# Wide row-maximum folds, maxima scaled on ScalarE, output weights that carry the sub-norm gains, and other buffer counts in a hybrid attention block

## The chip, the core and the metric

The kernel runs on one core of a Trainium2 chip. The metric is the device time of one launch in microseconds (us). Five engines work side by side, each through its own queue in order: TensorE (PE; its weight loads are shown apart as PEld), VectorE (DVE), ScalarE (ACT), GpSimd (POOL) and SyncE (SP), whose queue issues nearly all DMAs of this kernel. An engine whose next instruction waits holds up everything behind it in its queue.

## What is computed

One decoder layer on x (2048 tokens by 1024). h = RMSNorm(x), and one input projection of h is split into three attention branches and a gate z:

```
proj = rms_norm(x, norm_g) @ w_in
cq, ckv, kr, dq, dk, dv, mq, z = split(proj)
y_mla  = latent attention, 8 heads, 64 + 32 rotary columns, causal
y_diff = differential attention, 4 heads of two causal maps each:
         o = (softmax(q1 k1) - lam * softmax(q2 k2)) v
         y_diff = rms_norm(o, diff_subln_g) * (1 - lam_init)
y_mem  = attention over 256 memory tokens, 4 heads
x + (concat(y_mla, y_diff, y_mem) * silu(z)) @ w_out
```

Everything is float32 in the reference. The kernel keeps most operands as two float16 parts (a high part and what is left), so that a product takes three matmuls.

## The kernel before

The 2048 tokens are 16 tiles of 128, in 4 blocks of 4 tiles. The work is cut into steps: "m" (memory attention, 4 blocks), "d" (differential attention, 2 groups of 2 heads by 4 blocks) and "a" (latent attention, 4 groups of 2 heads by 4 blocks). A step has a preparation (projection, norms, rotary embedding, high and low parts, transposes by DMA) and the attention maps. A map goes over key tiles j: score matmuls into the PSUM tile `st`, Exp on ScalarE into the float32 tile `p32` (L493), the low part of it on VectorE into `plo` (L494), and then probability-by-value matmuls that read the upper halves of `p32` (L503, L505) and, one key tile later, `plo` (L523). `p32` has 3 buffers and `plo` has 4.

Softmax needs a maximum per query row that is subtracted. It isn't exact here: `est_block` computes scores of the high parts alone, takes row maxima of them, and puts the maximum divided by -32 as one more column into the query tile `qs` (L408), which is transposed a second time into `qB` (L471, L886). For block 0 the maximum is reduced straight from PSUM (L389). For blocks 1 to 3 ScalarE copies each score tile to bfloat16, the first key chunk into `er` (L391), the others into `ec` (L394), VectorE takes the running maximum (L395), and after every two query tiles folds 512 columns down to 64 by three halvings (L399) and reduces these (L400). `er` is two query tiles wide, with two buffers; `ec` has three.

The sources of all DMA transposes share one tag `s2`, 6 buffers (the function `stack`): the high and low parts of x, the query and key parts `qa`, `s`, `ks`, `qs` and the latents. The transposed queries `qB` have 5 buffers. Scratch tiles of 4 KB per partition share the tag `t4` with 2 buffers (`tmp4`); they go round in the order in which the program asks for them. `rope_tables` takes two of them, after three small tiles of its own for the positions and frequencies, which its first DMA (L254) fills.

After a "d" step `post_d` normalises the 64 columns of each head: squares on ScalarE with sums (L583), (sum + eps)^-0.5 on GpSimd (L97, L101), the product with it (L588) and with the gain row `g_sub` (L589), and then the gate (L592). `load_wout` loads w_out in 8 chunks of 128 rows, scales it by 64 and splits it in high and low parts (L926, L927); chunks 4 and 5 hold the rows of the "d" branch.

What sets the order: the generators of preparations, fillers and attention units are interleaved by due times, and each instruction gets a priority from that. A scheduler then lays the instructions of each engine in the order of a simulated run, in which a tile is handed out when a buffer of its tag is free. So the order on an engine depends on the durations in that simulation, and buffer counts change the order.

Of the kernel before, what the change touches and what calls it, by code (L numbers as in the profile page):

```python
# [11 lines left out]
F32 = mybir.dt.float32  # L12
F16 = mybir.dt.float16
BF16 = mybir.dt.bfloat16
I32 = mybir.dt.int32
# [4 lines left out]
P = 128  # L20
# [7 lines left out]
WS = 64.0  # L28
# [4 lines left out]
def _bc(ap, axis, n):  # L33
    ap = ap.unsqueeze(axis)
    shape = list(ap.shape)
    shape[axis] = n
    return ap.broadcast_to(shape)
# [3 lines left out]
def hybrid_block(ctx: ExitStack, tc: tile.TileContext, x, mem, positions, norm_g, w_in, mla_q_norm_g,  # L41
# [14 lines left out]
    ps_v = ctx.enter_context(tc.tile_pool(name="ps_v", bufs=1, space=bass.MemoryType.PSUM))  # L56

    def stack(shape, name):
        return wk.tile(shape, F16, tag="s2", name=name, bufs=6)

    def bigt(shape, name):
        return big.tile(shape, F16, tag="big", name=name)
# [20 lines left out]
    def gain_row(src, n, name):  # L83
        t = cst.tile([P, n], F32, name=name)
        SP.dma_start(t, src.broadcast_to([P, n]))
        return t
# [4 lines left out]
    def rstd_of(ss, shape, name, tag="rstd"):  # L91
        r = sm.tile([P, 32 if tag == "rstd" else 8], F32, tag=tag, name=name)
        n = int(np.prod(shape))
        rv = r[:, 0:n]
        if len(shape) == 2:
            rv = rv.rearrange("p (a b) -> p a b", b=shape[1])
        G.tensor_scalar(rv, ss, EPS, None, ALU.add)  # L97
        m = mhalf
        if len(shape) == 2:
            m = m.unsqueeze(2)  # L100
        G.tensor_tensor(rv, rv, m.broadcast_to([P] + list(shape)), ALU.pow)  # L101
        return rv
# [88 lines left out]
    def tmp4(name):  # L191
        return wk.tile([P, 1024], F32, tag="t4", name=name, bufs=2)
# [57 lines left out]
    sin_t = cst.tile([P, NT, 16], F32, name="sin_t")  # L250

    def rope_tables():
        pos_i = wk.tile([P, NT], I32, tag="posi", name="pos_i")
        SP.dma_start(pos_i, positions[0].rearrange("(t p) -> p t", p=P))  # L254
        pos_f = wk.tile([P, NT], F32, tag="posf", name="pos_f")
        V.tensor_copy(pos_f, pos_i)
        inv = np.float32(10000.0) ** (-np.arange(0, 32, 2, dtype=np.float32) / np.float32(32))
        inv_t = wk.tile([P, 16], F32, tag="invt", name="inv_t")
        for i in range(16):
            G.memset(inv_t[:, i:i + 1], float(inv[i]))  # L260
        w1 = tmp4("rp1")
        w2 = tmp4("rp2")
        ang = w1[:, 0:256]
        k = w1[:, 256:512]
        h = w1[:, 512:768]
        r = w1[:, 768:1024]
        a3 = ang.rearrange("p (t f) -> p t f", f=16)
        V.tensor_tensor(a3, _bc(pos_f, 2, 16), _bc(inv_t, 1, NT), ALU.mult)
        magic = 12582912.0
        V.tensor_scalar(k, ang, 1.0 / math.pi, magic, ALU.mult, ALU.add)  # L270
        V.tensor_scalar_sub(k, k, magic)
        p1 = 201.0 / 64.0
        p2 = math.pi - p1
        e2 = 2.0 ** (math.floor(math.log2(p2)) - 10)
        p2 = math.floor(p2 / e2) * e2
        p3 = math.pi - p1 - p2
        V.scalar_tensor_tensor(r, k, -p1, ang, ALU.mult, ALU.add)
        V.scalar_tensor_tensor(r, k, -p2, r, ALU.mult, ALU.add)
        V.scalar_tensor_tensor(r, k, -p3, r, ALU.mult, ALU.add)
        V.tensor_scalar(h, k, 0.5, -0.25, ALU.mult, ALU.add)  # L280
        V.tensor_scalar_add(h, h, magic)
        V.tensor_scalar_sub(h, h, magic)
        V.scalar_tensor_tensor(h, h, -2.0, k, ALU.mult, ALU.add)
        V.tensor_scalar(h, h, -2.0, 1.0, ALU.mult, ALU.add)
        V.scalar_tensor_tensor(w2[:, 0:256], r, -1.0, r, ALU.mult, ALU.max)
        A.activation(w2[:, 256:512], r, AF.Sin)
        A.activation(w2[:, 512:768], w2[:, 0:256], AF.Sin, scale=-1.0, bias=halfpi)
        V.tensor_tensor(sin_t.rearrange("p t f -> p (t f)"), w2[:, 256:512], h, ALU.mult)
        V.tensor_tensor(cos_t.rearrange("p t f -> p (t f)"), w2[:, 512:768], h, ALU.mult)
# [4 lines left out]
    g_k = gain_row(mla_kn_g, 96, "g_k")  # L294
    g_n = cst.tile([P, 64], F32, name="g_n")
    V.tensor_tensor(g_n, g_q[:, 0:64], g_k[:, 0:64], ALU.mult)
    g_sub = gain_row(diff_subln_g, 64, "g_sub")
    V.tensor_scalar_mul(g_sub, g_sub, (1.0 - LAM_INIT) / WS)
    lamw = tmp4("lamw")
    lamt = lamw[:, 0:128].rearrange("p (a b) -> p a b", b=32)  # L300
    SP.dma_start(lamt.rearrange("p a b -> p (a b)"), diff_lambda.rearrange("o a b -> o (a b)").broadcast_to([P, 128]))
# [72 lines left out]
    def est_block(st, i, nmap, mcol, lhs, rhs):  # L374
        b = st.b
        mx = sm.tile([P, nmap, 4, 2], F32, tag="mx", name=f"mx{i}_{st.name}", bufs=2)
        fold = b >= EB
        for m in range(nmap):
            for t in range(4):
                if fold and t % 2 == 0:  # L380
                    er = wk.tile([P, 2, 512], BF16, tag="er", name="er", bufs=2)
                for c in range(b + 1):
                    ps = ps_e.tile([P, 512], F32, tag="pe", name="pe")
                    n = (4 if c < b else t + 1) * P
                    T.matmul(ps[:, 0:n], lhsT=lhs(m, t), rhs=rhs(m, c, n // P), start=True, stop=c < b)  # L385
                    if c == b:
                        T.matmul(ps[:, t * P:n], lhsT=ident, rhs=mask_e, start=False, stop=True)  # L387
                    if not fold:
                        V.reduce_max(mx[:, m, t, c:c + 1], ps[:, 0:n], axis=AX.X)  # L389
                    elif c == 0:  # L390
                        A.activation(er[:, t % 2], ps, AF.Copy)  # L391
                    else:
                        ec = wk.tile([P, 512], BF16, tag="ec", name="ec", bufs=3)
                        A.activation(ec[:, 0:n], ps[:, 0:n], AF.Copy)  # L394
                        V.tensor_tensor(er[:, t % 2, 0:n], er[:, t % 2, 0:n], ec[:, 0:n], ALU.max)  # L395
                    yield 0.5
                if fold and t % 2:
                    for n in (256, 128, 64):
                        V.tensor_tensor(er[:, :, 0:n], er[:, :, 0:n], er[:, :, n:2 * n], ALU.max)  # L399
                    V.reduce_max(mx[:, m, t - 1:t + 1, 0], er[:, :, 0:64], axis=AX.X)  # L400
        if b == 1 and not fold:
            mr = sm.tile([P, nmap * 4], F32, tag="mr", name=f"mr{i}_{st.name}", bufs=2)
            V.reduce_max(mr, mx.rearrange("p m t c -> p (m t) c"), axis=AX.X)
            mr = mr.rearrange("p (m t) -> p m t", t=4)
        else:
            mr = mx[:, :, :, 0]
        for m in range(nmap):
            V.tensor_scalar_mul(mcol(m), mr[:, m, :], -1.0 / MS)  # L408


    def prep_d(st, units):
# [63 lines left out]
    class Map:  # L475
# [9 lines left out]
        def head(self, j):  # L485
            t0 = max(0, j - self.diag0)
            n = (4 - t0) * P
            ps = ps_s.tile([P, 512], F32, tag="st", name="st")
            self.scores(ps, j, t0, n, j >= self.diag0)
            p32 = wk.tile([P, 512], F32, tag="p32", name="p32", bufs=3)  # L490
            plo = wk.tile([P, 512], F16, tag="plo", name="plo", bufs=4)
            phi = p32.bitcast(BF16).rearrange("p (n t) -> p n t", t=2)[:, :, 1]
            A.activation(p32[:, :n], ps[:, :n], AF.Exp, scale=self.scale)  # L493
            V.tensor_tensor(plo[:, :n], p32[:, :n], phi[:, :n], ALU.subtract)  # L494
            return t0, phi, plo
# [81 lines left out]
    def post_d(st, y):  # L577
        y8 = y.rearrange("p t h d -> p (t h) d")
        ss = sm.tile([P, 8], F32, tag="yss", name=f"yss_{st.name}")
        ys = new_ys(4 + st.g, st.b)  # L580
        sink = ys[:, 0].rearrange("p t k -> p (t k)")
        for i in range(8):
            A.activation(sink[:, 64 * i:64 * i + 64], y8[:, i, :], AF.Square, scale=1.0 / 8.0, accum_out=ss[:, i:i + 1])  # L583
        yield 1.0
        r = rstd_of(ss[:, 0:8], [8], f"yr_{st.name}", "rstd_y")
        yield 1.0
        yield 1.0
        V.tensor_tensor(y8, y8, _bc(r, 2, 64), ALU.mult)  # L588
        V.tensor_tensor(y8, y8, _bc(g_sub, 1, 8), ALU.mult)  # L589
        yield 1.0  # L590
        yf = y.rearrange("p t h d -> p t (h d)")
        V.tensor_tensor(yf, yf, st.z, ALU.mult)  # L592
        yield 1.0
        yield from finish(st, yf, 4 + st.g, ys)
# [325 lines left out]
    def load_wout(cs):  # L920
        for c in cs:
            f = wk.tile([P, 1024], F32, tag="f4", name=f"f_wo{c}", bufs=2)
            SP.dma_start(f, w_out[0, c * P:(c + 1) * P, :])
            yield 1.0
            wt = bigt([P, 2, 1024], f"wo{c}")
            A.activation(wt[:, 0, :], f, AF.Copy, scale=WS)  # L926
            V.scalar_tensor_tensor(wt[:, 1, :], f, WS, wt[:, 0, :], ALU.mult, ALU.subtract)  # L927
            wout[c] = wt
            yield 1.0

# [318 lines left out]
```

## Time and profile before

| what | value |
|---|---|
| time, median of 3 runs | 1398.42 us (1397.34 to 1401.3) |
| time of the profiled execution | 1403.92 us |
| its span, first to last instruction | 1402.0 us |
| instructions | 35085 |
| busy PE / DVE / ACT / POOL | 93% / 79% / 64% / 25% |
| mean granted TensorE clock | 0.978 |
| chain that ended last, by engine | PE 59%, DVE 13%, DMA 10%, POOL 6%, ACT 5% |

Busy shares are of the span. Ends of matmuls are modelled in the profile, since matmuls overlap, so a busy PE is not a PE at its peak. A group of instructions is told as "line engine operation out<-in shapes xcount | busy us, mean ns of one | idle us of the engine before them, and what ended it".

### The profile page before, as it was taken

The page shows a single profiled execution, that of the slowest core. Times are in us where ns is not written, and L with a number is a line of the kernel's source. Part 1 is how long each engine was busy: PE and PEld are TensorE (multiplying, and loading weights), DVE is VectorE, ACT ScalarE, POOL GpSimd, SP SyncE. Part 2 cuts the span into 40 slices and gives each one's busy share as a digit, 9 for nine tenths or more (in the row PEclk, how much of TensorE's full clock was granted, in tenths as well). Part 3 has the DMA queues.
Part 4 walks back from the last instruction along what each step waited for, and adds up shares of the span by engine and source line. Part 5 has one row for each costly group of instructions (what it writes and reads, how often), then busy time and mean ns, then how long its engine had stood idle before and what let it go on. Part 6 is the DMA issues. An engine that isn't in the chain of part 4 may idle for free.

```text
span 1402.0 us, 35085 instructions
## 1 busy us (share of the span) xinstructions
PE 1303.8 (93%) x13552; PEld 830.8 (59%) x13552; DVE 1111.0 (79%) x2649; ACT 898.9 (64%) x2153; POOL 352.1 (25%) x541
## 2 busy tenths in 40 slices
PE   4789899999989999998998899999998898999998
PEld 1344456667678666666675656656655665655554
DVE  3458787989799858887897888978898899975645
ACT  5646443778786747775885767756776797763521
POOL 2222133304043033104113143353333503200000
PEclk9999999999999999999999999999999999999999
DMA  8999764144133123347255266535545353265462
GB/s 206 247 218 198 163 121 98 39 81 80 43 54 77 40 39 61 74 118 186 93 103 140 42 148 144 123 86 148 122 95 111 83 107 68 48 117 177 116 214 71
DMA packets 302695, 157.66 MB, mean 112 GB/s; under 512 B 248384, under 2 KB 281280, under 8 KB 302528
## 3 DMA queue, kind: packets, MB, share of 16 engines
q1 hardware_dynamic: 302496, 155.42, 48.7%
q8 instruction: 106, 1.74, 0.5%
q14 instruction: 61, 0.50, 0.1%
q0 software_dynamic: 32, 0.00, 0.0%
HBM read 61.79 MB, written 34.34 MB: 69 GB/s over the span
## 4 chain that ended last, share of the span: by engine, by line
PE 59%; DVE 13%; DMA 10%; POOL 6%; ACT 5%; issue 4%; SPq 2%; ACTq 0%; DVEq 0%; POOLq 0%
PE pp L176 6%; PE pp L177 6%; PE pp L178 6%; PE pe L385 6%; PE pv L505 4%; PE pv L503 3%; DVE plo L494 3%; PE pv L523 3%; PE pp L943 3%; PE pp L945 3%; PE pp L944 3%; DMA qB_a<-qs_a 3%; PE st L559 3%; PE st L903 3%; PE st L904 2%
## 5 line engine op out<-in xcount | busy, mean ns | idle before, releaser
L493 ACT ACTIVATE p<-st 128x512 f32<-128x512 f32 (+3 forms) x672 | 356.3, 548 | 210.3 <-PE st L905 81.4
L494 DVE TENSOR_TENSOR plo<-p 128x512 f16<-128x512 f32 (+3 forms) x672 | 406.3, 618 | 70.3 <-ACT p L493 67.8
L394 ACT ACTIVATE ec<-pe 128x512 bf16<-128x512 f32 (+3 forms) x384 | 196.1, 538 | 29.5 <-PE pe L387 11.7
L503 PEld LDWEIGHTS <-p 128*128 128x128 bf16 x2304 | 185.6, 100 | 48.6 <-DVE y_d L566 7.4
L505 PEld LDWEIGHTS <-p 128*128 128x128 bf16 x2304 | 172.3, 98 | 39.9 <-issue 2.9
L395 DVE TENSOR_TENSOR er<-er,ec 128x512 bf16<-128x512 bf16 (+3 forms) x384 | 143.0, 375 | 28.7 <-ACT ec L394 24.1
L523 PEld LDWEIGHTS <-plo 128*128 128x128 f16 x2304 | 120.8, 98 | 24.6 <-DVE plo L494 12.8
L391 ACT ACTIVATE er<-pe 128x512 bf16<-128x512 f32 x192 | 118.0, 617 | 24.0 <-PE pe L385 20.7
L176 PEld LDWEIGHTS <-ht_x 128*128 128x128 f16 x896 | 88.6, 99 | 72.2 <-DMA ht_x<-xh_x 20.9
L903 PE MATMUL st<-qB_a,kT_a 97*128 97x512 f16 (+1 forms) x320 | 113.4, 354 | 11.2 <-ACT p L493 10.2
L178 PEld LDWEIGHTS <-ht_x 128*128 128x128 f16 x896 | 88.7, 99 | 55.6 <-DMA ht_x<-xl_x 4.9
L177 PEld LDWEIGHTS <-ht_x 128*128 128x128 f16 x896 | 88.7, 99 | 54.2 <-issue 7.5
L503 PE MATMUL pv<-V_d,p 128*128 128x65 f16 x1088 | 115.8, 194 | 5.3 <-DVE y_d L566 3.9
L559 PE MATMUL st<-qB_d,kT_d 97*128 97x512 f16 (+1 forms) x320 | 112.0, 353 | 5.4 <-ACT p L493 4.7
L505 PE MATMUL pv<-V_d,p 128*128 128x64 f16 x1088 | 115.8, 196 | 0.0
L904 PE MATMUL st<-qB_a,kT_a 96*128 96x512 f16 (+1 forms) x320 | 112.9, 353 | 0.0
L905 PE MATMUL st<-qB_a,kT_a 96*128 96x512 f16 (+1 forms) x320 | 111.9, 350 | 0.0
L503 PE MATMUL pv<-V_a,p 128*128 128x65 f16 x1088 | 111.0, 193 | 0.0
L505 PE MATMUL pv<-V_a,p 128*128 128x64 f16 x1088 | 110.8, 195 | 0.0
L385 PE MATMUL pe<-kT_d,qB_d 96*128 96x512 f16 (+2 forms) x320 | 102.9, 350 | 5.8 <-DMA qB_d<-s_d 2.8
L385 PE MATMUL pe<-kT_a,qB_a 96*128 96x512 f16 (+2 forms) x320 | 93.6, 349 | 12.4 <-DMA qB_a<-qs_a 8.6
L176 PE MATMUL pp<-w_d,ht_x 128*128 128x512 f16 x256 | 97.0, 379 | 0.3 <-ACT ql L185 0.3
(285 smaller groups left out, 3335.2 us busy)
## 6 DMA issues: line engine op xcount, KB each, us to landing
xt_x<-in_x_dram SPq DMA_DIRECT2D x16, 512.0 KB, 4.8
xr<-in_x_dram SPq DMA_DIRECT2D x16, 512.0 KB, 3.8
part<-xr SPq DMA_DIRECT2D x16, 512.0 KB, 2.9
ysc<-yt SPq DMA_DIRECT2D x31, 256.0 KB, 2.0
yl<-ysc SPq DMA_DIRECT2D x15, 512.0 KB, 4.3
zsc<-zc SPq DMA_DIRECT2D x48, 128.0 KB, 2.3
xa<-part SPq DMA_DIRECT2D x12, 512.0 KB, 3.8
out_dram<-xa SPq DMA_DIRECT2D x12, 512.0 KB, 3.2
```

The source lines that it names most:

```text
L176: T.matmul(ps[:, :n], lhsT=ht[:, 0, k], rhs=wt[:, 0, :n], start=(k == 0), stop=False)
L177: T.matmul(ps[:, :n], lhsT=ht[:, 0, k], rhs=wt[:, 1, :n], start=False, stop=False)
L178: T.matmul(ps[:, :n], lhsT=ht[:, 1, k], rhs=wt[:, 0, :n], start=False, stop=(k == NK - 1))
L385: T.matmul(ps[:, 0:n], lhsT=lhs(m, t), rhs=rhs(m, c, n // P), start=True, stop=c < b)
L394: A.activation(ec[:, 0:n], ps[:, 0:n], AF.Copy)
L493: A.activation(p32[:, :n], ps[:, :n], AF.Exp, scale=self.scale)
L494: V.tensor_tensor(plo[:, :n], p32[:, :n], phi[:, :n], ALU.subtract)
L503: T.matmul(pvv[:, t, 0:65], lhsT=phi[:, c], rhs=vt[:, 0:65], start=(j == 0 and t == 0), stop=False, skip_group_check=True)
L505: T.matmul(pvv[:, t, 0:64], lhsT=phi[:, c], rhs=vt[:, 65:129], start=False, stop=False, skip_group_check=True)
L523: last["pv"] = T.matmul(pvv[:, t, 0:65], lhsT=plo[:, c], rhs=vt[:, 0:65], start=False, stop=(j == self.njt - 1), skip_group_check=True)
L559: T.matmul(ps[:, :n], lhsT=st.kTs[j // 4][0:97, h, j % 4, m % 2, :], rhs=st.qB[h][0:97, t0:4, m % 2, :], start=True, stop=not diag)
L903: T.matmul(ps[:, :n], lhsT=kt[0:97, h, j % 4, 0, :], rhs=q[0:97, 0, t0:4, :], start=True, stop=False)
```

## The change

Five things are edited together. (1) `er` becomes one tile for four query tiles with one buffer: the three folds and the reduction run once for four query tiles, on twice the width. (2) The maxima are scaled by -1/32 with a ScalarE copy in place of a VectorE multiplication. (3) The gain of the sub-norm and its factor move from `post_d` into chunks 4 and 5 of w_out, as a column `g_wo`; the 1/64 that was in the gain row becomes one GpSimd multiplication of 8 columns. (4) Buffers: `s2` 6 to 5, `p32` 3 to 4, `ec` 3 to 4. (5) `rope_tables` puts positions and frequencies into free columns of its second scratch tile and asks for both scratch tiles first.

```diff
--- before.py
+++ after.py
@@ -56,7 +56,7 @@
     ps_v = ctx.enter_context(tc.tile_pool(name="ps_v", bufs=1, space=bass.MemoryType.PSUM))
 
     def stack(shape, name):
-        return wk.tile(shape, F16, tag="s2", name=name, bufs=6)
+        return wk.tile(shape, F16, tag="s2", name=name, bufs=5)
 
     def bigt(shape, name):
         return big.tile(shape, F16, tag="big", name=name)
@@ -250,16 +250,16 @@
     sin_t = cst.tile([P, NT, 16], F32, name="sin_t")
 
     def rope_tables():
-        pos_i = wk.tile([P, NT], I32, tag="posi", name="pos_i")
+        w1 = tmp4("rp1")
+        w2 = tmp4("rp2")
+        pos_i = w2[:, 768:784].bitcast(I32)
         SP.dma_start(pos_i, positions[0].rearrange("(t p) -> p t", p=P))
-        pos_f = wk.tile([P, NT], F32, tag="posf", name="pos_f")
+        pos_f = w2[:, 784:800]
         V.tensor_copy(pos_f, pos_i)
         inv = np.float32(10000.0) ** (-np.arange(0, 32, 2, dtype=np.float32) / np.float32(32))
-        inv_t = wk.tile([P, 16], F32, tag="invt", name="inv_t")
+        inv_t = w2[:, 800:816]
         for i in range(16):
             G.memset(inv_t[:, i:i + 1], float(inv[i]))
-        w1 = tmp4("rp1")
-        w2 = tmp4("rp2")
         ang = w1[:, 0:256]
         k = w1[:, 256:512]
         h = w1[:, 512:768]
@@ -294,8 +294,10 @@
     g_k = gain_row(mla_kn_g, 96, "g_k")
     g_n = cst.tile([P, 64], F32, name="g_n")
     V.tensor_tensor(g_n, g_q[:, 0:64], g_k[:, 0:64], ALU.mult)
-    g_sub = gain_row(diff_subln_g, 64, "g_sub")
-    V.tensor_scalar_mul(g_sub, g_sub, (1.0 - LAM_INIT) / WS)
+    g_wo = cst.tile([P, 1], F32, name="g_wo")
+    for i in range(2):
+        SP.dma_start(g_wo[64 * i:64 * i + 64, :], diff_subln_g[0].rearrange("(p o) -> p o", o=1))
+    V.tensor_scalar_mul(g_wo, g_wo, (1.0 - LAM_INIT) * WS)
     lamw = tmp4("lamw")
     lamt = lamw[:, 0:128].rearrange("p (a b) -> p a b", b=32)
     SP.dma_start(lamt.rearrange("p a b -> p (a b)"), diff_lambda.rearrange("o a b -> o (a b)").broadcast_to([P, 128]))
@@ -377,8 +379,8 @@
         fold = b >= EB
         for m in range(nmap):
             for t in range(4):
-                if fold and t % 2 == 0:
-                    er = wk.tile([P, 2, 512], BF16, tag="er", name="er", bufs=2)
+                if fold and t == 0:
+                    er = wk.tile([P, 4, 512], BF16, tag="er", name="er", bufs=1)
                 for c in range(b + 1):
                     ps = ps_e.tile([P, 512], F32, tag="pe", name="pe")
                     n = (4 if c < b else t + 1) * P
@@ -388,16 +390,16 @@
                     if not fold:
                         V.reduce_max(mx[:, m, t, c:c + 1], ps[:, 0:n], axis=AX.X)
                     elif c == 0:
-                        A.activation(er[:, t % 2], ps, AF.Copy)
+                        A.activation(er[:, t], ps, AF.Copy)
                     else:
-                        ec = wk.tile([P, 512], BF16, tag="ec", name="ec", bufs=3)
+                        ec = wk.tile([P, 512], BF16, tag="ec", name="ec", bufs=4)
                         A.activation(ec[:, 0:n], ps[:, 0:n], AF.Copy)
-                        V.tensor_tensor(er[:, t % 2, 0:n], er[:, t % 2, 0:n], ec[:, 0:n], ALU.max)
+                        V.tensor_tensor(er[:, t, 0:n], er[:, t, 0:n], ec[:, 0:n], ALU.max)
                     yield 0.5
-                if fold and t % 2:
-                    for n in (256, 128, 64):
-                        V.tensor_tensor(er[:, :, 0:n], er[:, :, 0:n], er[:, :, n:2 * n], ALU.max)
-                    V.reduce_max(mx[:, m, t - 1:t + 1, 0], er[:, :, 0:64], axis=AX.X)
+            if fold:
+                for n in (256, 128, 64):
+                    V.tensor_tensor(er[:, :, 0:n], er[:, :, 0:n], er[:, :, n:2 * n], ALU.max)
+                V.reduce_max(mx[:, m, :, 0], er[:, :, 0:64], axis=AX.X)
         if b == 1 and not fold:
             mr = sm.tile([P, nmap * 4], F32, tag="mr", name=f"mr{i}_{st.name}", bufs=2)
             V.reduce_max(mr, mx.rearrange("p m t c -> p (m t) c"), axis=AX.X)
@@ -405,7 +407,7 @@
         else:
             mr = mx[:, :, :, 0]
         for m in range(nmap):
-            V.tensor_scalar_mul(mcol(m), mr[:, m, :], -1.0 / MS)
+            A.activation(mcol(m), mr[:, m, :], AF.Copy, scale=-1.0 / MS)
 
 
     def prep_d(st, units):
@@ -487,7 +489,7 @@
             n = (4 - t0) * P
             ps = ps_s.tile([P, 512], F32, tag="st", name="st")
             self.scores(ps, j, t0, n, j >= self.diag0)
-            p32 = wk.tile([P, 512], F32, tag="p32", name="p32", bufs=3)
+            p32 = wk.tile([P, 512], F32, tag="p32", name="p32", bufs=4)
             plo = wk.tile([P, 512], F16, tag="plo", name="plo", bufs=4)
             phi = p32.bitcast(BF16).rearrange("p (n t) -> p n t", t=2)[:, :, 1]
             A.activation(p32[:, :n], ps[:, :n], AF.Exp, scale=self.scale)
@@ -583,10 +585,10 @@
             A.activation(sink[:, 64 * i:64 * i + 64], y8[:, i, :], AF.Square, scale=1.0 / 8.0, accum_out=ss[:, i:i + 1])
         yield 1.0
         r = rstd_of(ss[:, 0:8], [8], f"yr_{st.name}", "rstd_y")
+        G.tensor_scalar(r, r, 1.0 / WS, None, ALU.mult)
         yield 1.0
         yield 1.0
         V.tensor_tensor(y8, y8, _bc(r, 2, 64), ALU.mult)
-        V.tensor_tensor(y8, y8, _bc(g_sub, 1, 8), ALU.mult)
         yield 1.0
         yf = y.rearrange("p t h d -> p t (h d)")
         V.tensor_tensor(yf, yf, st.z, ALU.mult)
@@ -923,8 +925,9 @@
             SP.dma_start(f, w_out[0, c * P:(c + 1) * P, :])
             yield 1.0
             wt = bigt([P, 2, 1024], f"wo{c}")
-            A.activation(wt[:, 0, :], f, AF.Copy, scale=WS)
-            V.scalar_tensor_tensor(wt[:, 1, :], f, WS, wt[:, 0, :], ALU.mult, ALU.subtract)
+            s = g_wo if c in (4, 5) else WS
+            A.activation(wt[:, 0, :], f, AF.Copy, scale=s)
+            V.scalar_tensor_tensor(wt[:, 1, :], f, s, wt[:, 0, :], ALU.mult, ALU.subtract)
             wout[c] = wt
             yield 1.0
```

## Rows read from the trace of the kernel before

**Rows 1.** The page's first part: busy us (share) and instruction count of each engine.
```profile
PE 1303.8 (93%) x13552; PEld 830.8 (59%) x13552; DVE 1111.0 (79%) x2649; ACT 898.9 (64%) x2153; POOL 352.1 (25%) x541
```
**Rows 2.** Windows: start:end, length, busy us by engine, PE clock, DMA share, GB/s.
```profile
0.00:250.00 250.00, 214.04 (x1413) 108.89 (x1414) 165.67 (x333) 129.00 (x254) 64.21 (x126) 0.96 0.80 175
100.00:150.00 50.00, 42.75 (x270) 20.91 (x268) 37.79 (x73) 28.13 (x50) 12.55 (x19) 0.90 1.01 196
250.00:1250.00 1000.00, 943.98 (x10854) 642.93 (x10852) 861.88 (x2153) 721.31 (x1808) 287.85 (x415) 0.98 0.42 92
```
**Rows 3.** The page's fourth part: the chain that ended last, by engine.
```profile
PE 59%; DVE 13%; DMA 10%; POOL 6%; ACT 5%; issue 4%; SPq 2%; ACTq 0%; DVEq 0%; POOLq 0%
```
**Rows 4.** Groups of VectorE instructions by line and shape.
```profile
L399 DVE TENSOR_TENSOR er<-er 128x512 bf16<-128x512 bf16 x96 | 41.1, 428 | 1.1
L399 DVE TENSOR_TENSOR er<-er 128x256 bf16<-128x256 bf16 x96 | 29.3, 305 | 0.7
L399 DVE TENSOR_TENSOR er<-er 128x128 bf16<-128x128 bf16 x96 | 21.3, 222 | 0.6
L400 DVE TENSOR_REDUCE mx_d<-er 128x2 f32<-128x128 bf16 x48 | 13.3, 277 | 0.4
...
L841 DVE TENSOR_REDUCE ss_a<-sqq_a 128x4 f32<-128x256 f32 x16 | 6.5, 409 | 0.3 <-ACT sqq_a L840 0.3
...
L408 DVE TENSOR_SCALAR qs_a<-mx_a 128x4 f16<-128x4 f32 x32 | 5.7, 179 | 0.2
L408 DVE TENSOR_SCALAR s_d<-mx_d 128x4 f16<-128x4 f32 x32 | 5.7, 178 | 0.2
L589 DVE TENSOR_TENSOR y_d<-y_d,g_sub 128x512 f32<-128x512 f32 x8 | 5.6, 697 | 0.0
```
**Rows 5.** Groups of ScalarE instructions of L394, widest and narrowest shape.
```profile
L394 ACT ACTIVATE ec<-pe 128x512 bf16<-128x512 f32 x240 | 143.2, 618 | 19.4 <-PE pe L385 10.2 <-PE pe L387 4.8 <-DVE er L395 1.7
...
L394 ACT ACTIVATE ec<-pe 128x128 bf16<-128x128 f32 x48 | 14.0, 291 | 4.7 <-PE pe L387 2.2 <-PE pv L523 2.0 <-DVE er L395 0.3
```
**Rows 6.** A GpSimd group: the eps addition of the sub-norm.
```profile
L97 POOL TENSOR_SCALAR yr_d<-yss_d 128x8 f32<-128x8 f32 x8 | 5.5, 682 | 41.4 <-ACT ys L583 41.2
```
**Rows 7.** Waits: engine line <- releaser: us in total, times, longest us.
```profile
POOL ks_a L866 <- DMA qB_a<-qs_a: 57.3, 7, 17.5
...
ACT p L493 <- PE pv L505: 26.2, 21, 4.9
```
**Rows 8.** Timeline of SP's queue at the start: start us, duration us, instruction.
```profile
4.47 0.43 SPq L254 DMA_DIRECT2D pos_i<-in_positions_dram  x1
4.95 5.10 SPq L85 DMA_DIRECT2D g_mk<-in_mem_kn_g_dram  x1
...
12.07 1.34 SPq L136 DMA_TRANSPOSE ht_x<-xh_x  x1
```
**Rows 9.** The chain in order of time: the same issue stands in it.
```profile
4.95 5.10 SPq L85
```
**Rows 10.** Timeline of VectorE, start to 127 us: first low part, the rotary tables, block 2.
```profile
8.78 1.28 DVE L138 SCALAR_TENSOR_TENSOR xl_x<-xt_x,r_x,xh_x 128x1024 f16<-128x1024 f32 x1 [0.86 <-ACT xh_x L134]
...
11.37 0.17 DVE L256 CAST pos_f<-pos_i 128x16 f32<-128x16 int32 x1 [0.64 <-DMA pos_i<-in_positions_dram]
...
102.70 0.42 DVE L268 TENSOR_TENSOR rp<-pos_f,inv_t 128x256 f32<-128x256 f32 x1
...
109.69 0.68 DVE L628 TENSOR_TENSOR qa_m<-qn_m,qa_m 128x512 f16<-128x512 f32 x1
...
116.41 0.42 DVE L289 TENSOR_TENSOR cos_t<-rp,rp 128x256 f32<-128x256 f32 x1
...
125.86 1.21 DVE L613 TENSOR_REDUCE ss_m<-sq_m 128x16 f32<-128x1024 f32 x1
```
**Rows 11.** Timeline of ScalarE: a query part of the third "a" group is written.
```profile
1013.62 0.52 ACT L873 ACTIVATE qs_a<-qkv_a 128x384 f16<-128x384 f32 x1 [0.27 <-DVE qkv_a L861]
```
**Rows 12.** Timeline of SP's queue: the first transpose of that query part.
```profile
1065.52 1.23 SPq L877 DMA_TRANSPOSE qB_a<-qs_a  x1
```

## The prediction, made before the changed kernel was run

> **What bounds the kernel now.** I read the page's first part, then windows, then the chain that ended last, then the groups of the edited lines, then the waits. TensorE is busy 93% of the span and VectorE 79% [rows 1]. The windows show where TensorE is not busy: 250 - 214.0 = 36.0 us in the first 250 us, where the DMA engines run at 80%, and 1000 - 944.0 = 56.0 us in the 1000 us in which maps and preparations run side by side [rows 2]. In that stretch VectorE is busy 862 of 1000 us and ScalarE 721. Nothing the change touches takes a matmul away, so what it can win is idle time of TensorE: at most the 56 us, and something at the start. The chain says which work ends late: 59% PE, 13% DVE, 5% ACT, 6% POOL [rows 3]. I use it as an exchange rate. DVE has 0.13 x 1402 = 182 us on the chain and 1111 us of busy time, so a us of VectorE work stands for 182 / 1111 = 0.164 us of span. For ACT it is 70 / 899 = 0.078, for POOL 84 / 352 = 0.24.
>
> All terms are made against the profiled execution, 1403.92 us with a span of 1402.0; it lies 5.5 us above the median of the runs, 1398.42, and I take the difference over to that median.
>
> **Folds.** L399 and L400 run 96 times each, that is 48 times for four query tiles. Now four tiles cost 2 x (428 + 305 + 222 + 277) = 2464 ns [rows 4]. The wide fold starts with twice the width of the widest row. The slope from 128 to 512 columns is (428 - 222) / 384 = 0.536 ns a column, so 1024 columns cost 428 + 512 x 0.536 = 703 ns; then 428 and 305, which are rows; the reduction of 256 columns is 409 ns by the row of L841, which is float32 [rows 4]. Sum 1845 ns, a saving of 619 ns x 48 = 29.7 us of VectorE. Bounds: nothing, if each wide instruction costs twice the narrow one, and 59 us, if it costs the same as the narrow one; I take the slope, since it comes from the same line.
>
> **Maxima on ScalarE.** 32 x 179 + 32 x 178 ns = 11.4 us leave VectorE [rows 4]. ScalarE gets 64 copies of 4 columns: slope (618 - 291) / 384 = 0.85 ns a column, 291 - 124 x 0.85 = 186 ns, 11.9 us in all [rows 5]. So the work isn't less, it moves from the fuller to the emptier engine. The Trainium skill speaks against it: its page ScalarE: Activation LUTs, Rules for kernel authors, sends multiplications to VectorE; the same page (What ACT_TABLE_LOAD costs) gives 186 ns and 0.833 ns a column, an estimate of 189 ns here, so trace and page agree on the price. If that rule decided, the move would be a loss, and the sum below would end 1.9 us higher. Behind the moved copy stand Exps and score copies of the same queue, and it waits for the reduction on VectorE; the second transpose (L471, L886) waits for it.
>
> **Sub-norm gain.** 8 x 697 = 5.6 us leave VectorE [rows 4]. GpSimd gets 8 multiplications of 8 columns, 8 x 682 = 5.5 us by the nearest row [rows 6]. The scaling of w_out by a column in place of a constant I cost at nothing, since two chunks of eight are touched and the chunks are loaded long before use; its cover gone, it would cost a chunk's ScalarE copy.
>
> Together VectorE loses 29.7 + 11.4 + 5.6 = 46.7 us. At 0.164 this is **-7.7 us**; bounds 0 and -46.7. ScalarE's 11.9 us at 0.078 are **+0.9** (bounds 0 and 11.9), GpSimd's 5.5 at 0.24 **+1.3** (0 and 5.5).
>
> **p32 with four buffers.** ScalarE waits 26.2 us for L505, the last reader of a `p32` buffer, in 21 pieces [rows 7]. That goes. What is late next is the score tile in PSUM, which has two buffers as before. At 0.078 the gain is **-2.0**; bounds 0 and -26.2. The fourth `ec` buffer I cost at nothing: the idle time before L394 that the running maximum L395 ends is 1.7 us at the widest shape [rows 5].
>
> **One wide er.** With one buffer the first copy of the next map (L391) can't start before the reduction of the last has ended, where two buffers let it run on. A fold is 1.85 us, so 48 x 1.85 = 88.6 us of ScalarE waiting at most. Behind it in the queue stand the Exps. The scheduler knows the wait and can put Exps ahead of it, so I take a quarter of it, and 0.078 of that: **+1.7**; bounds 0 and 88.6.
>
> **s2 from six to five.** GpSimd already waits 57.3 us for these buffers at L866 [rows 7], so a loss suggests itself. But a query part written at 1013.62 is transposed at 1065.52 only [rows 11, 12]: its `qB` (5 buffers) is freed by the scores of five query tiles earlier. A source waits in its buffer for a `qB`, and writing it later by one release moves nothing while 52 us lie between. I take **0**; bounds 0 and the 57.3 us again at POOL's rate, +13.8.
>
> **Rotary tables.** The DMA of the positions is issued at 4.47, and the next issue on SP lasts 5.10 us where that one took 0.43 [rows 8]; this stands in the chain [rows 9]. The first transposed x follows at 12.07, though its high part is there at 8.78, when VectorE starts on it [rows 8, 10]. In the change this DMA writes into the second `t4` tile, which is asked for behind the scratch of block 1 and can't be had before the last L628 of block 1 ends, 109.69 + 0.68 = 110.4 [rows 10]. So the start wins 12.07 - 8.78 = 3.3 us. At 110 SP stalls 4.7 us instead, and the tables come late: landing 11.37 - 4.47 = 6.9 us after the issue, then 116.83 - 102.70 = 14.1 us of work, ready at 131.4 where they were at 116.8. They hold both `t4` buffers, and the squares of block 2, summed at 125.86, need one; these slip by 131.4 - 124.8 = 6.6 us, counting a square of 1 us before. TensorE is idle 7.25 of 50 us there [rows 2], so of 4.7 + 6.6 = 11.3 us I charge 7.25 / 50: 1.6. Net **-1.7**; bounds -3.3 and +11.3.
>
> **Sum.** -7.7 + 0.9 + 1.3 - 2.0 + 1.7 + 0 - 1.7 = -7.5 us: a profiled 1396.4, and 1398.42 - 7.5 = 1390.9, said as 1391.
>
> **Rivals.** What tells no change from a change here is about 0.3%, 4.2 us: faster is below 1394.2, slower above 1402.6.
> A (0.42): the sum, with its own range 1384 to 1397 from terms halved or half as large again.
> B (0.22): VectorE's work lies beside matmuls, the late ends shift to the next thing in line, and it stays at 1398. For it: the large share of PE in the chain, and L399 and L400 start with nearly no idle before them [rows 3, 4].
> C (0.14): VectorE is the bound of the long stretch and half of the 56 us go, 1398.4 - 28 = 1370. For it: 862 of 1000 us busy. Against it: 13% of the chain. [...]
> D (0.16): the one `er` is the new wait. Score copies stop at each of the 48 folds, the three PSUM tiles of the estimates fill, and TensorE's queue, in order, stands behind an estimate matmul. It decides from 48 x w = 7.5 + 1.7 = 9.2 us, w = 0.19 us a fold. At 0.4 us a fold it is 19 us, 1398.4 - 9.2 + 19.2 = 1408. Against it: 88.6 us of such waits is a bound that the scheduler sees and can order around.
> E (0.06): the late tables cost their whole 11.3 us and the start wins nothing: -5.8 + 11.3 = +5.5, 1404.
>
> Besides, the order on all engines is laid anew by the simulated run, since durations and buffers change; that can add some us of either sign to each case, and I widen for it.
>
> **Chances.** Faster: A without its upper edge 0.36, C 0.14, 0.02 of B: 0.52. Same: 0.06 of A, 0.17 of B, 0.01 of D: 0.24. Slower: D 0.15, E 0.06, 0.03 of B: 0.24. The range 1370 to 1409 takes C's and D's numbers in and leaves about 2 in 10 out.
>
> **What would show it.** In the changed profile: VectorE's busy time near 1064 us; 48 folds with steps near 0.70, 0.43, 0.31 and 0.41 us; ScalarE up by 12 us; no wait of Exp for L505; the positions issued near 110 us, the 5 us issue gone from 4.95 and the first matmul some 3 us earlier. D would show as ScalarE's L391 waiting for the reduction and TensorE's L385 for L391 or L394. The prediction is wrong if the idle time of TensorE in the long stretch stays at 56 us though VectorE's work is down (B), falls by tens of us (C), or grows (D); or if `ks` and `qs` begin to hold `qB` back, which I cost at nothing.

## The result, and the profile after

The changed kernel takes 1388.37 us (median of 8 runs, 1381.39 to 1394.8) beside 1397.93 us before (8 runs, 1393.63 to 1404.07). The ratio is 0.9923, with a 95% interval of 0.9897 to 0.9948: 0.8% faster, some 10 us. It is taken over the runs, not from the two medians. The prediction was 1391 us, the sum of rival A. The experiments below show that this sum came out right by luck. Its largest term, VectorE's saved work, has no fixed price and is worth about nothing in the kernel as changed; the buffer counts, costed at 2 us, give the whole gain by themselves.

The profiled execution after has a span of 1387.9 us, 14.1 less than the one before. Its page, first part, answers to [rows 1]; then come its windows, which answer to [rows 2], and the chain by engine, which answers to [rows 3].

```profile
PE 1295.6 (93%) x13552; PEld 829.7 (60%) x13552; DVE 1081.3 (78%) x2385; ACT 904.8 (65%) x2219; POOL 351.5 (25%) x549
```

```profile
0.00:250.00 250.00, 211.97 (x1436) 108.70 (x1437) 165.81 (x330) 132.91 (x268) 64.41 (x125) 0.97 0.79 176
100.00:150.00 50.00, 42.64 (x274) 20.64 (x273) 35.63 (x71) 30.71 (x53) 11.52 (x16) 0.97 0.87 174
250.00:1250.00 1000.00, 950.04 (x10956) 648.98 (x10953) 838.46 (x1916) 725.30 (x1863) 287.11 (x424) 0.98 0.42 94
```

```profile
PE 53%; DVE 15%; DMA 13%; ACT 7%; POOL 7%; issue 4%; SPq 1%; ACTq 0%; DVEq 0%; POOLq 0%
```

VectorE's busy time is 29.7 us lower, and TensorE's idle time in the long stretch (250 to 1250 us) falls from 56.0 to 50.0 us. VectorE's share of the chain did not fall with its work, it rose from 13 to 15%. That is the first sign against the prediction's exchange rate.

The groups of the edited lines (line numbers are 2 higher than before): the wide fold, its reduction, the scaling of the maxima on ScalarE, and GpSimd's new multiplication. They answer to [rows 4 to 6].

```profile
L401 DVE TENSOR_TENSOR er<-er 128x1024 bf16<-128x1024 bf16 x48 | 33.5, 698 | 0.4
L401 DVE TENSOR_TENSOR er<-er 128x512 bf16<-128x512 bf16 x48 | 20.3, 423 | 0.2
L401 DVE TENSOR_TENSOR er<-er 128x256 bf16<-128x256 bf16 x48 | 13.7, 286 | 0.3
L402 DVE TENSOR_REDUCE mx_a<-er 128x4 f32<-128x256 bf16 x24 | 9.9, 413 | 0.3
```

```profile
L410 ACT ACTIVATE s_d<-mx_d 128x4 f16<-128x4 f32 x32 | 7.3, 229 | 14.6 <-DVE mx_d L391 8.2 <-DVE mx_d L402 5.2 <-issue 0.9
L410 ACT ACTIVATE qs_a<-mx_a 128x4 f16<-128x4 f32 x32 | 7.0, 219 | 10.6 <-DVE mx_a L402 8.7 <-DVE mx_a L391 0.8 <-DMA zt_a<-zsc 0.8
```

```profile
L588 POOL TENSOR_SCALAR yr_d<-yr_d 128x8 f32<-128x8 f32 x8 | 2.6, 331 | 0.7
```

A fold of four query tiles takes 698 + 423 + 286 + 413 = 1820 ns, where 1845 were worked out.

The waits after, ScalarE's and GpSimd's, answer to [rows 7]. Behind GpSimd's stand the rows of the kernel before that [rows 7] leaves out.

```profile
ACT p L495 <- PE st L907: 71.2, 76, 5.4
...
ACT p L495 <- PE pv L507: 6.3, 8, 2.5
...
ACT er L393 <- DVE mx_d L402: 3.6, 5, 1.8
...
ACT p L495 <- DVE plo L496: 3.0, 5, 1.7
```

```profile
POOL qs_a L874 <- DMA qB_a<-qs_a: 87.0, 10, 20.3
POOL qs_a L874 <- DMA kT_a<-ks_a: 78.9, 13, 11.1
...
POOL ks_a L868 <- DMA qB_a<-qs_a: 43.8, 6, 13.3
...
POOL ks_a L868 <- DMA kT_a<-ks_a: 28.9, 11, 8.3
```

```profile
POOL qs_a L872 <- DMA kT_a<-ks_a: 54.4, 17, 9.0
...
POOL ks_a L866 <- DMA kT_a<-ks_a: 40.8, 9, 10.7
...
POOL qs_a L872 <- DMA qB_a<-qs_a: 39.4, 10, 13.2
```

The Exp's wait for the product with v falls from 26.2 to 6.3 us, and the first copy into the one `er` waits only 3.6 us for the reduction: rival D did not come. GpSimd's four rows of waits for a source buffer grow from 191.9 us in sum to 238.6, though the kernel is faster. The start, in SP's timeline, answers to [rows 8]; behind it stand two instructions of VectorE from the time of the positions:

```profile
4.46 0.47 SPq L85 DMA_DIRECT2D g_mk<-in_mem_kn_g_dram  x1
...
10.87 1.35 SPq L136 DMA_TRANSPOSE ht_x<-xh_x  x1
...
98.63 0.39 SPq L256 DMA_DIRECT2D rp<-in_positions_dram  x1
104.25 1.23 SPq L631 DMA_TRANSPOSE qA_m<-qa_m  x1
```

```profile
103.42 0.17 DVE L258 CAST rp<-rp 128x16 f32<-128x16 int32 x1 [4.28 <-DMA rp<-in_positions_dram]
103.53 0.69 DVE L630 TENSOR_TENSOR qa_m<-qn_m,qa_m 128x512 f16<-128x512 f32 x1
```

The 5.10 us issue is gone from the start, and the first transposed x comes 1.2 us earlier, not 3.3. The next issue behind the positions starts 5.6 us after theirs, but this is not the stall of the start: it transposes `qa_m`, which VectorE has written at 103.53 + 0.69 = 104.22 us, and VectorE stood 4.28 us waiting for the positions first.

### The profile page after: what moved, and what is told of

The parts are those of the page before. It is cut to its first block, busy times and chain, and to the rows that moved or that the text cites. A ratio compares the mean times of both kernels' runs of the same rounds, so it can differ in the third digit from the quotient of the medians.

```text
span 1387.9 us, 34839 instructions
## 1 busy us (share of the span) xinstructions
PE 1295.6 (93%) x13552; PEld 829.7 (60%) x13552; DVE 1081.3 (78%) x2385; ACT 904.8 (65%) x2219; POOL 351.5 (25%) x549
## 4 chain that ended last, share of the span: by engine, by line
PE 53%; DVE 15%; DMA 13%; ACT 7%; POOL 7%; issue 4%; SPq 1%; ACTq 0%; DVEq 0%; POOLq 0%
PE pp L176 6%; PE pp L178 6%; PE pp L177 6%; PE pe L387 5%; DVE plo L496 5%; DMA qB_a<-qs_a 3%; PE pv L507 3%; PE pv L505 3%; PE pp L946 3%; PE pv L525 3%; PE pp L948 3%; PE pp L947 3%; PE st L905 2%; PE st L906 2%; PE st L907 2%
## 5 line engine op out<-in xcount | busy, mean ns | idle before, releaser
L393 ACT ACTIVATE er<-pe 128x512 bf16<-128x512 f32 x192 | 114.5, 612 | 21.0 <-PE pe L387 17.2
L387 PE MATMUL pe<-kT_a,qB_a 96*128 96x512 f16 (+2 forms) x320 | 98.9, 358 | 12.7 <-DMA qB_a<-qs_a 9.7
L387 PE MATMUL pe<-kT_d,qB_d 96*128 96x512 f16 (+2 forms) x320 | 106.8, 349 | 3.0 <-DMA qB_d<-s_d 1.5
```

## The experiments

Theories, as the expectations name them. V: VectorE's saved work is the gain, 0.164 us of span for each us of it. S: the slack of the exponentials (`p32`) is the gain. W and D: the one wide `er` costs by its wait. C2: `p32` pays only beside a lighter VectorE. K: fewer `s2` help. O: the order laid anew moves the time whichever part is edited. Kernels named u_ are the changed kernel with one part undone, a_ the kernel before with some parts alone, q only the order laid anew, w_ the kernel before with other buffer counts. Every ratio is to the kernel before, run beside them.

**u_fold**, the folds narrow again.
```
-                if fold and t == 0:
-                    er = wk.tile([P, 4, 512], ..., bufs=1)
+                if fold and t % 2 == 0:
+                    er = wk.tile([P, 2, 512], ..., bufs=2)
...
```


> The changed kernel with the folds narrow again: two query tiles in one er tile, two buffers of it, the rest of the change kept. Theory V (VectorE's saved work is the gain, at 0.164 us of span for each us): VectorE's 48 folds take their 29.7 us again, so 4.9 us of the gain go and the time is 1388.4 + 4.9 = 1393.3, 0.9965 of before. Theory S (the Exp waits that the fourth p32 buffer took away are the gain): the time stays at 1388.4. Theory W (the single wide er holds something up, so that the wide fold costs part of what it saves): faster than 1388.4, by up to 5 us. Theory O (the order that is laid anew decides, whichever part is changed): several us of either sign, with the idle time of TensorE in the long stretch moving with no relation to VectorE's work.

Measured 1388.69 us, ratio 0.9929 (0.9906 to 0.9953). The time stays where it was, though VectorE is busier by 13.2 us, as its page says:
```profile
PE 1295.1 (93%) x13552; PEld 828.9 (60%) x13552; DVE 1094.5 (79%) x2577; ACT 907.2 (65%) x2219; POOL 357.2 (26%) x549
```
The largest saving of the change is worth nothing that can be measured beside the rest of it. V's 4.9 us don't show, and neither does W; with the two intervals together some 5 us either way, this run alone can't rule V out.

**u_max**, the maxima scaled on VectorE again.
```
-            A.activation(mcol(m), mr[:, m, :], AF.Copy, scale=-1.0 / MS)
+            V.tensor_scalar_mul(mcol(m), mr[:, m, :], -1.0 / MS)
```


> The changed kernel with the 64 maxima scaled on VectorE again. Theory V: VectorE gets 11.4 us back (+1.9 us of span), ScalarE loses 14.3 us (at 0.078, -1.1): 1389.2. If ScalarE's queue is what the copy disturbs (it waits 20 us in groups for the reduction on VectorE, with Exps and score copies behind it): faster, 1388.4 - 4 = 1384. Theory S: 1388.4. Theory O: several us of either sign.

Measured 1393.49 us, ratio 0.9968 (0.9947 to 0.9989): 5 us slower than the changed kernel, where V expected 0.8. Whether it is the edit or the order stays open (see the two runs of the order alone).

**u_p32**, three `p32` buffers.
```
-            p32 = wk.tile([P, 512], F32, tag="p32", name="p32", bufs=4)
+            p32 = wk.tile([P, 512], F32, tag="p32", name="p32", bufs=3)
```


> The changed kernel with three p32 buffers. Theory S: the waits of the Exp for the product with v come back (26 us before) and most of the gain goes, 1388.4 + 7 = 1395 or more. Theory V: only the 2.0 us that the prediction gave to this part go, 1390.4. If the wait only moves to the score tiles in PSUM: 1388.4, with the Exp's idle time unchanged in sum. Theory O: several us of either sign.

Measured 1401.15 us, ratio 1.001 (0.999 to 1.003). The whole gain is gone, with all of VectorE's saving still in place. Two of ScalarE's waits in this kernel:
```profile
ACT p L495 <- PE pv L507: 25.4, 19, 5.1
ACT p L495 <- DVE plo L496: 25.2, 34, 2.0
```
The Exp waits 25.4 us for the products with v, and 25.2 us for `plo`, VectorE's subtraction, which reads the same buffer; these rows were 6.3 and 3.0 us with four buffers.

**u_rope**, the positions in tiles of their own, read at the start.
```
-        pos_i = w2[:, 768:784].bitcast(I32)
+        pos_i = wk.tile([P, NT], I32, tag="posi", name="pos_i")
...
```


> The changed kernel with the positions in tiles of their own, so that their DMA is issued at the start again. By the prediction's term of -1.7 us: 1390.1, with the 5 us issue at about 5 us again and the first matmul some 2 us later. By the trace of the changed kernel, in which the start is 1.9 us earlier at the first matmul but most of that lead is gone by 115 to 200 us: no difference, 1388.4. Rival E (the late tables cost more than the start wins): faster, 1388.4 - 5 = 1383. Theory O: several us of either sign.

Measured 1392.11 us, ratio 0.9954 (0.9935 to 0.9973). The sign is the prediction's; the size, 3.7 us, is inside what the order alone moves.

**q48_after and q52_after**, the order alone (0.52 in the second).
```
-                    yield 0.5
+                    yield 0.48
```


> The changed kernel with not one instruction, tile or buffer changed: only the planner's cost of a step of the estimates is 0.48 in place of 0.50, so that the order on the engines is laid anew. This measures theory O by itself. If the order is worth nothing, 1388.4 within 1.5 us. If it is worth several us, 1383 to 1394, and then differences of 4 to 5 us between the variants (the scaling of the maxima, the rotary tables) can't be put down to the edited part.

> The same with 0.52 in place of 0.50. The same expectations: 1388.4 within 1.5 us if the order is worth nothing; anything from 1383 to 1394 if it is worth several us. A value near that of the kernel with three p32 buffers (1401) would say that even this could be the order's work.

Measured 1389.63 us, ratio 0.9932 (0.9914 to 0.9949), and 1392.64 us, ratio 0.995 (0.9935 to 0.9966). Neither one has another instruction or buffer than the changed kernel. So these two new orders move the kernel by up to some 4 us. u_rope lies inside that, u_max just past it; u_p32, with 12.8 us, is far outside. Two orders are no bound, though.

**a_s5p4**, the two buffer counts alone on the kernel before.
```
-        return wk.tile(shape, F16, tag="s2", name=name, bufs=6)
+        return wk.tile(shape, F16, tag="s2", name=name, bufs=5)
...
-            p32 = wk.tile([P, 512], F32, tag="p32", name="p32", bufs=3)
+            p32 = wk.tile([P, 512], F32, tag="p32", name="p32", bufs=4)
```


> The kernel before with one edit of the change alone: s2 with five buffers and p32 with four (the fourth does not fit beside six s2). Theory S (the fourth p32 buffer is the main part of the gain: taking it from the changed kernel cost 1401.2 - 1388.4 = 12.8 us, all of the gain): 1398.4 - 9 = 1389, with the Exp's wait for the product with v down from 26 us to about 6. Theory V (VectorE's saved work): 1398.4 - 2.0 = 1396. Theory C2 (p32 pays only together with a lighter VectorE, since a p32 buffer is also held by plo on VectorE): 1398, and the folds and maxima alone are worth nothing either. Theory O (the order that is laid anew decides): within some 5 us of 1398 on either side.

Measured 1387.64 us, ratio 0.9911 (0.989 to 0.9933): two edited numbers are as fast as the whole change, and the fourth `ec` buffer isn't needed for it. C2 falls, since VectorE's work is that of before. Of ScalarE's waits, the one for the product with v did not fall to 6 us as expected:
```profile
ACT p L493 <- PE pv L505: 19.6, 17, 2.6
...
ACT p L493 <- DVE plo L494: 5.4, 9, 1.4
```
So the us of this row are not the price. The longest single piece fell from 4.9 us [rows 7] to 2.6.

**a_fmg**, VectorE's three parts alone (folds, maxima, sub-norm gain), with three `p32` and six `s2`; the diff is that of the change without its buffer counts and rotary tables.

> The kernel before with VectorE's three parts of the change alone: wide folds, maxima on ScalarE, sub-norm gain in w_out; s2, p32, ec and the tables as before. Theory V: 46.7 us of VectorE's work at 0.164 less what ScalarE and GpSimd get, 1398.4 - 5.5 = 1393, and by the first comparisons no less than the 5 us that the maxima seemed to be worth. Theory S: 1398.4, with the Exp's wait for the product with v at its 26 us. Theory C2: 1398.4. Theory O: within some 5 us of 1398 on either side.

Measured 1409.89 us, ratio 1.0073 (1.0049 to 1.0097). It is slower than before, though its page shows 25 us less VectorE:
```profile
PE 1304.6 (93%) x13552; PEld 831.0 (59%) x13552; DVE 1085.8 (77%) x2385; ACT 901.2 (64%) x2217; POOL 352.8 (25%) x549
```
V, as a fixed rate, fails with this in sign.

**a_s5**, five `s2` alone.
```
-        return wk.tile(shape, F16, tag="s2", name=name, bufs=6)
+        return wk.tile(shape, F16, tag="s2", name=name, bufs=5)
```


> The kernel before with five s2 buffers in place of six and nothing else. The comparison with five s2 and four p32 (0.9911) left open which of the two counts did it. Theory S (the fourth p32 buffer): 1398.9, within the 4 us by which an order laid anew moves the time. Theory K (one source buffer fewer holds preparations back and leaves the queues freer for the maps): 1388. Bound from the prediction for the loss by fewer s2: up to +13.8, 1412.

Measured 1416.47 us, ratio 1.0114 (1.009 to 1.0139). Every theory missed; only the prediction's upper bound, 13.8 us, comes near the 17 measured. Two of GpSimd's waits for source buffers, in this kernel and in a_s5p4, the one with four `p32`:
```profile
POOL qs_a L872 <- DMA kT_a<-ks_a: 104.9, 18, 11.6
...
POOL ks_a L866 <- DMA qB_a<-qs_a: 88.5, 11, 13.9
```
```profile
POOL qs_a L872 <- DMA kT_a<-ks_a: 66.3, 14, 9.9
...
POOL ks_a L866 <- DMA qB_a<-qs_a: 47.8, 9, 12.3
```
They were 54.4 and 57.3 us before. But the four rows of GpSimd's waits for a source buffer together are 191.9 us before, 239.5 here, 220.0 in a_s5p4 and 238.6 in the changed kernel, which is 2% faster than a_s5. So they rose with the fewer sources, and their sum is not the loss. From a_s5 to a_s5p4 the one `p32` buffer takes 28.8 us away; in the changed kernel it is worth 12.8. What the buffer is worth depends on what stands around it.

The same holds for VectorE's work. u_p32 is a_s5 with the other parts of the change put in (folds, maxima, gain, tables and `ec`), and it is 14.5 us faster by the ratios (1.0010 beside 1.0114). So these parts gain with three `p32` and five `s2`, where folds, maxima and gain lose 10 us with three and six (a_fmg), and all of them come to nothing with four and five (0.9923 beside 0.9911). How much of the 14.5 us is VectorE's work, and how much the order, no run separates.

The profiled execution of a_s5 has a span 6.2 us longer than that of the kernel before (its time, 1409.97 us, is the lowest of the five runs). It falls behind between 1150 and 1203 us: up to there it has made 11123 matmuls beside 11099, and in that stretch 471 beside 578. The windows of the stretch, before and in a_s5, then a stall of TensorE inside it, and the windows over the stall and behind it:
```profile
1150.00:1203.00 53.00, 47.03 (x578) 29.75 (x576) 51.03 (x121) 40.15 (x94) 21.94 (x30) 1.00 0.35 69
```
```profile
1150.00:1203.00 53.00, 43.37 (x471) 28.43 (x470) 46.55 (x110) 34.03 (x86) 22.83 (x37) 0.87 0.36 75
```
```profile
1179.86 0.20 PE L503 MATMUL pv<-V_a,p 128*128 128x65 f16 x1 [2.15 <-DVE y_a L910]
```
```profile
1177.70:1179.80 2.10, 0.00 (x1) 0.00 (x0) 2.10 (x6) 0.32 (x2) 2.10 (x5) 1.00 0.00 0
1180.10:1183.40 3.30, 3.30 (x46) 2.48 (x42) 3.30 (x8) 2.00 (x5) 2.24 (x4) 0.50 0.20 40
1184.00:1188.00 4.00, 4.00 (x57) 2.75 (x55) 4.00 (x11) 1.19 (x2) 0.00 (x0) 1.00 0.34 65
```
TensorE stands idle for 2.15 us until VectorE's `y_a`, then its granted clock is 0.50, 1.2 in place of 2.4 GHz, for at least 3.3 us, and then it is 1.00 again. This stall is paid twice: 2.15 us of idle time and, as an estimate, half of the 3.3 us behind it. TensorE is busy for the whole 3.3 us, so the sums of busy time hide the second part. Not every stall is followed by a lower clock. Here is one of 2.4 us in the same run, and the 3.4 us behind it:
```profile
837.70:840.10 2.40, 0.00 (x1) 0.00 (x0) 0.49 (x2) 1.04 (x3) 0.48 (x3) 1.00 1.11 207
840.10:843.50 3.40, 3.21 (x23) 1.96 (x23) 2.97 (x11) 3.40 (x10) 0.21 (x1) 1.00 1.00 317
```
How the fewer sources lead to such a stall was not followed.

**q48_before**, the order alone on the kernel before; the edit is that of q48_after.

> The kernel before with no instruction, tile or buffer changed: only the planner's cost of a step of the estimates is 0.48 in place of 0.50. Theory O (the order alone can do it, and the kernel before had an unlucky one): 1390 or less. Theory S (three p32 buffers hold whatever order is laid): 1395 to 1403. If the mean clock of the runs rises from 0.978 to 0.985 without the fourth buffer, the clock is the order's and not the buffer's.

Measured 1400.45 us, ratio 1.0012 (0.9998 to 1.0026). The mean clock of its runs stays at 0.978. This is weaker than its counterpart, since the edit moved fewer instructions: 12685 of 13552 matmuls keep their place in TensorE's order, beside 6450 in q48_after. So it does not bound what another order could do with three buffers.

**a_fold**, the wide folds alone on the kernel before; the diff is that of the change at these lines.

> The kernel before with the wide folds in one er tile alone; three p32, six s2, maxima on VectorE. The three VectorE parts together made the kernel before slower by 0.7% (1409.9). Theory D (the single er is a wait that costs more than the fold saves as long as p32 is short): 1405 to 1410, with ScalarE's first copies waiting longer for the reduction than in the kernel before. Theory V: 1398.9 - 4.9 = 1394. If the maxima or the gain made the loss: 1399.

Measured 1408.45 us, ratio 1.0062 (1.004 to 1.0083), what D expected, and D's wait is there; it was 1.8 us before, for both tiles:
```profile
ACT er L391 <- DVE mx_a L400: 9.0, 10, 2.5
...
ACT er L391 <- DVE mx_d L400: 5.3, 8, 2.4
```
It is 14.3 us in all, and no proof of D: in a_fmg the same wait is 2.0 us and the loss is as large.

**w_s4p5l5**, more slack for the exponentials still, on the kernel before.
```
-        return wk.tile(shape, F16, tag="s2", name=name, bufs=6)
+        return wk.tile(shape, F16, tag="s2", name=name, bufs=4)
...
-            p32 = wk.tile([P, 512], F32, tag="p32", name="p32", bufs=3)
-            plo = wk.tile([P, 512], F16, tag="plo", name="plo", bufs=4)
+            p32 = wk.tile([P, 512], F32, tag="p32", name="p32", bufs=5)
+            plo = wk.tile([P, 512], F16, tag="plo", name="plo", bufs=5)
```


> The kernel before with s2 at four buffers, p32 at five and plo at five, to see whether the slack of the exponentials is worth more than one buffer. Theory S continued: the fourth p32 gave 11 us, a fifth gives half of that again, 1383. If the two score tiles in PSUM are what the Exp waits for next (it waits for them 160 us in sum with four buffers): 1388, no more than with four. If four s2 hold the transposes back (GpSimd's and ScalarE's waits for kT and qB grow): 1392 to 1400.

Measured 1399.0 us, ratio 0.9989 (0.9969 to 1.0008). A fifth `p32` and a fifth `plo`, paid for with an `s2`, give the gain back; which of the three counts does it was not tried. No version here beats the changed kernel measurably; a_s5p4 equals it.

## All runs side by side

Each run has its span and its mean granted clock. Span x (1 - clock) is an estimate, on the high side, of the time lost to the lower clock, since TensorE isn't busy in all of it (56.9 of 64.8 us in the profile of the kernel before); the rest is the span less that. Means over the runs of each kernel (66 of the kernel before, from three comparisons), us:

```
               p32  s2  ratio   span    lost to clock  rest
a_s5p4          4    5  0.9911  1385.0  19.4           1365.6
after           4    5  0.9923  1386.1  25.1           1361.0
u_fold          4    5  0.9929  1387.3  21.9           1365.4
q48_after       4    5  0.9932  1387.8  19.0           1368.8
q52_after       4    5  0.9950  1390.7  19.2           1371.5
u_rope          4    5  0.9954  1390.4  21.8           1368.6
u_max           4    5  0.9968  1392.5  17.8           1374.8
w_s4p5l5        5    4  0.9989  1396.5  22.7           1373.8
before          3    6  1       1397.4  30.9           1366.5
u_p32           3    5  1.0010  1398.8  21.7           1377.1
q48_before      3    6  1.0012  1398.4  31.1           1367.3
a_fold          3    6  1.0062  1406.0  28.9           1377.0
a_fmg           3    6  1.0073  1408.2  28.4           1379.7
a_s5            3    5  1.0114  1412.5  33.1           1379.5
```

The count of `p32` sorts the kernels: seven with four buffers lie at 0.9911 to 0.9968, six with three at 1 to 1.0114. VectorE's work doesn't: the fastest one has the narrow folds, and three of the six slow ones have the wide. For a_s5p4 nearly all of the 12.4 us by which its mean span is shorter is clock by this estimate (11.5 us); for the changed kernel about half is (5.8 of 11.3). But the clock doesn't go with `p32` alone: u_p32, with three, loses 21.7 us to it and is as slow as the kernel before. Where the higher clock comes from stays open.

## Why the prediction was right, point by point

The time was right by luck: two terms were wrong in opposite directions, and the sign of the change was never VectorE's.

- **VectorE's work, -7.7.** The instructions came out as worked out: 1820 for 1845 ns a fold, and the 46.7 us taken away are 46.7 us in the sum of durations. In busy time it is 29.7 us, since neighbouring instructions overlap in the records (1276.5 us summed are 1111.0 us busy, before) and busy time counts the overlap once. The step that failed is the exchange rate. A us of VectorE was to be worth 182 / 1111 of a us; with the folds undone nothing measurable came back (u_fold), alone the work saved went with a loss (a_fold, a_fmg), and beside three `p32` and five `s2` it went with a gain (u_p32 beside a_s5). There is no one rate. The share of an engine in the chain says where the chain went, and not what goes when work leaves it: `plo` alone had 3% of the chain before and has 5% after.
- **Rival B** (VectorE's work lies beside matmuls) fits the kernels with four `p32`, with the wrong time, since it had no other gain; it doesn't fit the 14.5 us between a_s5 and u_p32. **C** falls with the time itself, 1388 for 1370, and with a_fmg.
- **p32, -2.0.** Mis-sized: 12.8 us in the changed kernel, 28.8 in the kernel before with five `s2`, past the bound of 26.2. The prediction took the row's 26.2 us at ScalarE's rate. A path that would make it dearer is that the Exp stands ahead of score copies and of `plo`, and TensorE's products wait for that `plo`; this is argued and not shown. No row of these sizes could be read off before. The fourth `ec`, costed at nothing, was not tried by itself.
- **s2, 0.** Mis-sized: 17.3 us alone (a_s5, 1416.47 beside 1399.2). The argument was one source with 52 us between its writing and its transpose. It said nothing of the other sources: GpSimd's wait at L872 for `kT` rose from 54.4 to 104.9 us in the profiles. Whether the change pays this loss too isn't shown: from a_fmg to u_p32 the `s2` go from six to five, with the tables and `ec` edited beside them, and the time falls (1.0073 to 1.0010). Four `p32` beside six `s2` don't fit into the core's memory, so this was not tried.
- **ScalarE, +0.9, and the one er, +1.7.** 219 to 229 ns for 186: 14.3 us, not 11.9. The `er` wait is 3.6 us in the changed kernel, for 88.6 as a bound. D's time, 1408, is near a_fold's 1408.45 with three `p32`; a_fmg loses as much without D's wait, and beside four there is no loss.
- **GpSimd, +1.3.** 2.6 us for 5.5; the gain in w_out was not tried by itself.
- **Rotary tables, -1.7.** The start won 1.9 us at the first matmul (16.15 to 14.25), not 3.3, since the transposed x then stands behind other issues and waits 0.7 us for a load of x. The positions were issued at 98.6 and not at 110. SP's 4.7 us stall behind them wasn't seen: the next issue waited for `qa_m`, and VectorE stood 4.28 us for the positions. The tables were ready at 135.4, not 131.4, and the squares of block 2 were summed 13.1 us later, not 6.6; TensorE's idle time from 100 to 150 us stayed at 7.4 us for 7.25, so this cost nothing there. Undone, +3.7 us with the order's scatter on it: not settled.
- **The signs named.** VectorE's busy time was to come near 1064 us and came to 1081.3; the idle time of TensorE fell, which spoke for A over B, D and E, and yet VectorE's work was not why.
- **The sum.** -7.7 - 2.0 + 0 was read as mostly VectorE; the two counts alone give -12, and VectorE's work added to them about 0. The two errors cancel.

What stays open: which chain through ScalarE, VectorE and TensorE the fourth buffer shortens, why the parts gain or lose by the buffers beside them, and how much of the 12 us a good order alone could give with three buffers.

## What to carry to other kernels

A buffer count in the stage that feeds TensorE can outweigh tens of us saved on an engine that runs beside it (here 12 us of span for two counts, about 0 for 46.7 us of VectorE's work added to them): try the counts alone before the arithmetic. Edits need not add up: a part undone in the changed kernel and the same part alone can differ in sign. The share of an engine in the chain of waits is no exchange rate for its work. Where a scheduler lays the order anew, measure what the order alone does (a planner's cost nudged, no instruction changed) before a few us are given to an edit.

## What was not expected of the hardware

- A stall can be paid twice: 2.15 us idle and then 1.2 GHz for at least 3.3 us (a_s5), though 2.4 us idle in the same run left the clock at 2.4 GHz. By the estimate above 17.8 to 33.1 us of the span are lost to the lower clock, as much as the differences under study.
- A copy of 4 columns on ScalarE takes 219 to 229 ns, above the 186 that the line through its 128 and 512 columns gives.
- At the start the issue behind the DMA of the positions lasts 5.10 us (5.43 in u_rope, which issues it there again). Moved to 98.6 us, that DMA shows no such issue behind it, as far as the wait for `qa_m` lets one see; VectorE stood 4.28 us for its data.
